# Attention in pairs of heads: three-pass scores issued in turn on the two 64-row halves of TensorE, in a two-block transformer on one core

## The chip, the core and the metric

The kernel runs on one core of a Trainium2 chip (trn2), in one launch. The metric is the device time of one execution in microseconds; the profiler's trace of one execution gives every instruction of the five engines: TensorE (PE, with its weight loads as PEld), VectorE (DVE), ScalarE (ACT), GpSimd (POOL) and SyncE (SP), which issues the transfers.

## The reference

Two transformer blocks of two layers each, in float32, on one sequence of 512 tokens of width 1024. The first block mixes a pooled branch, a convolved branch and dilated attention, then attends to a memory of 256 rows, then runs a gated MLP. The second attends with 512 tokens and 256 context rows; its layer 0 has grouped attention (A) and differential attention (B), its layer 1 windowed attention with a sink (C) and neighbourhood attention with a bias (D). Cut to the attention, all heads being 64 wide:

```python
def block(bi):                                   # block 1: 4 heads per group, 3 groups share one softmax
    for g, (window, dil) in enumerate(DIL_CONFIGS):
        sc = einsum("bhqd,bhqkd->bhqk", qb[g], kk) * scale
        ...
    wts = softmax(stack(lses, axis=0), axis=0)
    return sum(wts * stack(outs, axis=0), axis=0)
def gqa_attend(q, k, v):                         # A: 8 query heads on 2 key heads
    p = softmax(einsum('bqkgd,bskd->bkgqs', q, k), axis=-1)
    return einsum('bkgqs,bskd->bqkgd', p, v)
def diff_attend(q, k, v, lam):                   # B: 4 heads, two score maps each
    p = softmax(einsum('bqhjd,bshjd->bhjqs', q, k), axis=-1)
    return einsum('bhqs,bshe->bqhe', p[:, :, 0] - lam * p[:, :, 1], v)
# C: keys of 3 neighbouring blocks of 128 and the context, with a sink; D: 8 rows by 16 columns, with a bias
```

## The kernel before

Tokens lie in four blocks of 128 (`NB`), the context in two. Nearly all large products are made in three passes (`mm3`, lines 228 to 232): each operand is split into a part h and a rest l of type float32r, and h·h, l·h and h·l are added up in PSUM. These products are L230, L231 and L232 in the trace.

An attention is a list of **units** of three steps each, which `pipe` (line 401) puts into the program: `s` (scores and softmax, which leaves p [128 queries, keys] in SBUF), `t` (`keys_T`, line 380: TensorE transposes p in tiles of 128 into a PSUM tile of four, ACT or DVE copies it to SBUF) and `v` (`pv`, line 394: value products of two heads, one on each half of the array's columns). Before the change a unit is **one head** of one block of 128 queries; `lag` and `order` say how many units later its `t` and `v` follow. `mix` (line 77) lays other products, the fill, between the units, in a proportion from CONFIG: the gates of the first branch in block 1 (`gate_pass`), the projections of B beside A (`proj_b`), those of D beside C (`proj_d`), and beside B and D the first half of the output product (`out_first`), a token block of 24 products as soon as its attention is done. Tile's scheduler then puts the instructions of each engine into their final order.

A PSUM tile for scores, `wide` ([128, 1024], two buffers), holds one head. The scores are made in three ways:

- Block 1 (`attend`, lines 682 and 684), B (`attend_b` by `scores`, lines 1392, 1393 and, for context queries, 1395), the context's A (`attend_actx`, line 1470) and D (`attend_d` by `scores`): plain float32 products with 64 rows of contraction. A float32 product stands in the trace as two instructions.
- A and C (`s2`, lines 1336 and 1337): h and l of q lie stacked over the 128 rows, and meet a copy of h of k on both halves; then h of q meets l of k on 64 rows.

B and D differ in their softmax. In D two DVE passes (lines 1615 and 1618) add bias and mask, write p to SBUF and give the maximum; ACT takes the exponentials from p (line 360), DVE divides (lines 366 and 367). In B DVE reads the scores for the maximum (line 1507), ACT reads them once more for the exponentials (line 1510), DVE makes p0/d0 - lam·p1/d1 (lines 1511 to 1516). In B a second list of units, four of the context's A and then eight of the context's B, is interleaved one by one with the sixteen units of the tokens (`run`, line 1815).

Of the kernel before, what the change touches and what calls it, by code (L numbers as in the profile page):

```python
# [19 lines left out]
P = 128  # L20
D = 1024
# [13 lines left out]
CONFIG = dict(wm0=5,wm1=0,wm2=2,wm3=0,wm4=0,s1=16,s2=1,mixo0=20,mixo1=25,so=2,st=2,sf=8,d_e1=60,d_e2=60,shp=0,d_hn=25,eva=0,evb=0,evc=0,o1=0,om=0,oa=2,oc=3,evd=1, own=4, fa=40, fc=10, w1=2, slack=8, sm=4, sr=1, d_sub=110, mix1=125, mixm=130, laga=3, lagc=3, lag1=2, lagm=1, mixa=100, mixc=130, sz0=[6, 4, 4, 4, 4], sz1=[6, 4, 4, 4, 4], tick=60, bg=1500, d_mem=180, d_wmo=130, d_wout=180, d_in=60, d_ffn=80, d_op=60, d_opc=80, d_mlp=130, d_mlpc=120, d_last=140, d_ctx=100, d_rope=40, d_head=110, d_mod=100, raw=4, w=4, t4=6, a4=18, mm=4, wide=2)  # L35
# [23 lines left out]
class Act(list):  # L59
    """k-tiles (h, l) of an operand; ready(b) emits what token block b still waits for"""  # L60
# [16 lines left out]
def mix(main, fills, ahead=0.0):  # L77
    """runs main to its end; of each (gen, ratio) in turn about ratio microseconds for each of main's, after ahead of them"""
    fills = list(fills)
    b = 0.0  # L80
    while b < ahead:
        b += next(fills[0][0], ahead)
    a = b = 0.0
    for c in main:
        a += c
        while fills and b < fills[0][1] * a:
            d = next(fills[0][0], None)
            if d is None:
                fills.pop(0)
                a = b = 0.0  # L90
                break
            b += d


class Core:
    def __init__(self, nc, tc, es, I):
# [17 lines left out]
        self.spare, self.lent = [], {}  # L114
# [5 lines left out]
    def pe(self, us):  # L120
        """us of PE work were emitted; work that was put off until now follows"""
# [21 lines left out]
    def act(self, hl):  # L143
        """the k-tiles of a (h, l) pair of tiles whose blocks arrive under one key"""
# [14 lines left out]
    def t4(self, n=1024, dt=F32):  # L159
        if self.spare and n <= 768 and dt == F32:  # L160
            base = self.spare.pop(0)
            t = self.ap.tile([P, n], dt, tag="t4", name="t4", bufs=CONFIG["t4"]) if base is None else base[:, :n]
            self.lent[id(t)] = t, base
            return t
# [14 lines left out]
    def lend(self, tags=("hTh", "hTl")):  # L179
        """the memory of other tags as further t4 tiles; free() after their last use"""  # L180
        for tag in tags:
            t = self.ap.tile([P, 5, 768], F32, tag=tag, name=tag, bufs=1)
            self.spare += [t[:, i] for i in range(5)]
        self.spare += [None] * CONFIG["own"]

    def free(self, t):
        if id(t) in self.lent:
            self.spare.append(self.lent.pop(id(t))[1])

# [7 lines left out]
    def sm(self, n=1):  # L197
        return self.sp.tile([P, n], F32, tag=f"sm{n}", name=f"sm{n}", bufs=24 if n == 1 else 6)
# [15 lines left out]
    def w(self, src, k0, nk, c0, ncol):  # L214
        nc = self.nc
        raw = self.wp.tile([P, nk, ncol], F32, tag="wraw", name="wraw", bufs=CONFIG["raw"])
        nc.sync.dma_start(
            out=raw, in_=src[k0 * P:(k0 + nk) * P, c0:c0 + ncol].rearrange("(k p) n -> p k n", p=P)
        )
# [61 lines left out]
    def gained(self, y, g, out, eng=None):  # L281
        """(y * g, sum of squares of y over D) of one half"""
# [4 lines left out]
    def postnorm(self, x, parts):  # L287
        """x += rms(y) * g, the halves of y as gained() left them"""
# [10 lines left out]
    def fm(self, src, col, act, n=T):  # L299
        """feature-major product of one block of 128 columns: psum [128, n]"""  # L300
# [13 lines left out]
    def fm_halves(self, src, cols, act):  # L314
        """the same for several blocks of columns, the first half of the tokens before the second"""
# [12 lines left out]
    def tm_into(self, ps, ws, act, b):  # L328
        """token-major product of token block b: act[k] (h, l) [128, tokens], ws pieces of kpp k-tiles"""
# [9 lines left out]
    def tm_w(self, src, nk, c0, n):  # L339
        z = 2 if n > 256 else 4  # L340
        return [self.w(src, k, z, c0, n) for k in range(0, nk, z)]

    def tm(self, src, c0, n, acts, evac, between=None, ws=None):
        """acts: [(act, blocks, base)], in order"""
# [12 lines left out]
    def exp_norm(self, p, src, nmx, extra=None):  # L357
        nc = self.nc
        den = self.sm()
        nc.scalar.activation(p, src, AF.Exp, bias=nmx, scale=1.0, accum_out=den)  # L360
        if extra is not None:
            es = self.sm()
            nc.scalar.activation(es, extra, AF.Exp, bias=nmx, scale=1.0)
            nc.vector.tensor_add(den, den, es)
        rd = self.sm()
        nc.vector.reciprocal(rd, den)
        nc.vector.tensor_scalar(p, p, rd, None, op0=ALU.mult)

    def softmax2(self, p, S, nmx, den, n):
        """two rows of n keys side by side"""  # L370
# [9 lines left out]
    def keys_T(self, p, n):  # L380
        nc = self.nc
        pT = self.t4(n * P)
        for a in range(0, n, 4):
            b = min(a + 4, n)
            pt = self.ps1((b - a) * P)
            for m in range(a, b):
                nc.tensor.transpose(pt[:, blk(m - a)], p[:, blk(m)], self.ident)
            if a == 0 or self.evac:
                nc.scalar.copy(pT[:, a * P:b * P], pt)
            else:  # L390
                nc.vector.tensor_copy(pT[:, a * P:b * P], pt)
        return pT
# [1611 lines left out]
```

## Time and profile before

| | |
|---|---|
| time, median of 3 runs (lowest to highest) | 3663.67 us (3659.64 to 3666.01) |
| profiled execution, first to last instruction | 3659.7 us |
| what lies around that span in the median | 4.0 us |
| granted TensorE clock, mean | 0.989 of full |
| TensorE busy | 3557.6 us, 97% |
| VectorE, ScalarE, GpSimd busy | 2070.1, 1524.2, 490.7 us (57%, 42%, 13%) |
| transfers | 362.11 MB, 99 GB/s |

The page gives no separate time for the profiled execution; its span stands beside the median of the other runs. Matmuls are pipelined: one that is listed with 0.39 us may be followed by the next after 0.23 us, so what a matmul costs is read from the start of one to the start of the next. The attentions are five stretches of the span: block 1 at 152 us and 1113 us (two layers), A from 2019 us, B from 2164 us, C from 2983 us, D from 3136 us.

### The profile page before, as it was taken

How to read it: one execution, taken by the hardware profiler on the slowest of the kernel's cores; microseconds unless marked ns; L12 is line 12 of the kernel's file. 1: busy time of each engine (PE TensorE's matmuls, PEld its weight loads, DVE VectorE, ACT ScalarE, POOL GpSimd, SP SyncE). 2: the span in 40 equal slices, each digit the busy share in tenths (PEclk: the TensorE clock that was granted, in tenths of full speed). 3: DMA queues.
4: the chain of work that ended last, by engine and by line, in shares of the span. 5: the costliest groups of instructions: out<-in, count | busy, mean ns of one | idle time of the engine just before them, and what ended most of it. 6: DMA issues, size and time to landing. Idle time of an engine off the chain costs nothing. (4 is left out here: it accounts for less than half of the span.)

```text
span 3659.7 us, 47457 instructions
## 1 busy us (share of the span) xinstructions
PE 3557.6 (97%) x18504; PEld 2921.8 (80%) x18504; DVE 2070.1 (57%) x3329; ACT 1524.2 (42%) x2728; POOL 490.7 (13%) x463
## 2 busy tenths in 40 slices
PE   8999989999999999999999999999999999999999
PEld 7878878888797888888877776798888777668887
DVE  6655687576655436545676466644343664654445
ACT  4543455444544324443434454432222354554222
POOL 1222141123321011000023000200000110110000
PEclk9999999999999999999999999999999999999999
DMA  5434553444452234333441000322121320113332
GB/s 166 146 98 127 176 167 96 123 151 154 147 162 77 83 97 163 101 94 109 123 138 53 29 24 1 98 87 64 58 70 58 127 64 24 64 64 98 98 98 81
DMA packets 382096, 362.11 MB, mean 99 GB/s; under 512 B 20488, under 2 KB 297480, under 8 KB 381872
## 3 DMA queue, kind: packets, MB, share of 16 engines
q1 hardware_dynamic: 381872, 359.08, 31.2%
q8 instruction: 145, 2.38, 0.3%
q14 instruction: 79, 0.65, 0.1%
HBM read 347.34 MB, written 11.70 MB: 98 GB/s over the span
## 5 line engine op out<-in xcount | busy, mean ns | idle before, releaser
L225 DVE TENSOR_TENSOR wl<-wraw,wh 128x1024 fp32r<-128x1024 f32 (+2 forms) x499 | 612.0, 1231 | 616.4 <-ACT wh L221 613.4
L221 ACT CAST wh<-wraw 128x1024 fp32r<-128x1024 f32 (+2 forms) x504 | 510.2, 1016 | 789.1 <-PE mm L231 402.9
L230 PE MATMUL mm<-hTh,wh 128*128 128x512 f32 (+1 forms) x2112 | 785.7, 372 | 6.5 <-ACT hTh L237 4.4
L231 PE MATMUL mm<-hTl,wh 128*128 128x512 f32 (+1 forms) x2112 | 782.9, 371 | 2.0 <-DVE hTl L238 2.0
L232 PE MATMUL mm<-hTh,wl 128*128 128x512 f32 (+1 forms) x2112 | 782.7, 371 | 0.0
L230 PE MATMUL mm<-wh,a 128*128 128x512 f32 x1312 | 517.5, 395 | 3.0 <-DVE acc L1780 1.7
L231 PE MATMUL mm<-wl,a 128*128 128x512 f32 x1312 | 512.6, 391 | 1.1 <-DVE wl L225 1.1
L232 PE MATMUL mm<-wh,a 128*128 128x512 f32 x1312 | 511.7, 391 | 1.1 <-DVE a L238 1.1
L230 PEld LDWEIGHTS mm<-hTh,wh 128*128 128x128 f32 x2112 | 399.2, 189 | 76.6 <-ACT hTh L237 4.8
L232 PEld LDWEIGHTS mm<-hTh,wl 128*128 128x128 f32 x2112 | 399.7, 189 | 68.0
L231 PEld LDWEIGHTS mm<-hTl,wh 128*128 128x128 f32 x2112 | 399.8, 189 | 67.7 <-DVE hTl L238 2.4
L230 PEld LDWEIGHTS mm<-wh,a 128*128 128x128 f32 x1312 | 247.3, 189 | 62.4 <-issue 5.8
L232 PEld LDWEIGHTS mm<-wh,a 128*128 128x128 f32 x1312 | 246.9, 188 | 54.8 <-DVE a L238 2.9
L231 PEld LDWEIGHTS mm<-wl,a 128*128 128x128 f32 x1312 | 247.3, 188 | 51.6 <-DVE wl L225 2.2
L231 PE MATMUL mm<-wl,hTh 128*128 128x384 f32 (+2 forms) x640 | 226.5, 354 | 14.9 <-DVE wl L225 14.7
L230 PE MATMUL mm<-wh,hTh 128*128 128x384 f32 (+2 forms) x640 | 232.1, 363 | 4.0 <-ACT wh L221 2.5
L252 POOL TENSOR_TENSOR sm<-sm,mhalf 128x1 f32<-128x1 f32 (+3 forms) x112 | 83.6, 747 | 1097.5 <-DVE sm L248 783.3
L232 PE MATMUL mm<-wh,hTl 128*128 128x384 f32 (+2 forms) x640 | 226.0, 353 | 1.4 <-DVE hTl L238 1.4
L1096 ACT ACTIVATE t<-t,mod_s 128x512 f32<-128x512 f32 x168 | 119.7, 722 | 138.5 <-DVE macc L1092 69.3
L1097 POOL TENSOR_TENSOR t<-t,t 128x512 f32<-128x512 f32 x84 | 124.3, 1480 | 288.8 <-ACT t L1096 253.3
L1097 POOL TENSOR_TENSOR macc<-macc,t 128x512 f32<-128x512 f32 x84 | 120.9, 1440 | 311.8 <-ACT t L1096 257.8
L1780 DVE TENSOR_TENSOR acc<-acc,mm 128x512 f32<-128x512 f32 x112 | 76.8, 686 | 120.4 <-PE mm L232 120.2
(319 smaller groups left out, 5290.0 us busy)
## 6 DMA issues: line engine op xcount, KB each, us to landing
wraw<-in_w_in SPq DMA_DIRECT2D x108, 512.0 KB
t<-in_w_mod SPq DMA_DIRECT2D x96, 512.0 KB
wraw<-in_w_up SPq DMA_DIRECT2D x88, 512.0 KB
wraw<-in_w_mlp_in SPq DMA_DIRECT2D x64, 512.0 KB
wraw<-in_w_mlp_out SPq DMA_DIRECT2D x64, 512.0 KB
wraw<-in_w_down SPq DMA_DIRECT2D x44, 512.0 KB
a<-dr SPq DMA_DIRECT2D x38, 512.0 KB
wraw<-in_w_in SPq DMA_DIRECT2D x48, 384.0 KB
```

The source lines that it names most:

```text
L221: nc.scalar.copy(h, raw)
L225: eng.tensor_sub(l, raw, as32(h))
L230: mm(out, L[0], R[0], start=first, stop=False)
L231: mm(out, L[0], R[1], start=False, stop=False)
L232: mm(out, L[1], R[0], start=False, stop=last)
L252: nc.gpsimd.tensor_tensor(r, v, self.mhalf.to_broadcast([P, n]) if n > 1 else self.mhalf, op=ALU.pow)
L1096: nc.scalar.activation(w[:, kk], w[:, kk], AF.Copy, scale=sc)
L1097: nc.gpsimd.tensor_add(acc, acc, w[:, kk])
L1780: nc.vector.tensor_add(y, y, ps)
```

## The change

Heads are taken in pairs everywhere. A unit is now **two heads** (in B: the two score maps of one head), which lie on rows 0 to 63 and 64 to 127 of the array. Their scores are made in three float32r passes, for both in turn (`pair_scores`, the products at line 365 of the changed kernel), into both `wide` tiles. Both softmaxes, all their transposes (line 395; copies at lines 398, DVE, and 400, ACT) and their value products (line 409) belong to the one unit.

```diff
+    def pair_scores(self, S, segs):
+        for c0, n, q, k in segs:
+            for i, j in ((0, 0), (0, 1), (1, 0)):
+                for e in range(2):
+                    z = slice(64 * e, 64 * e + 64)
+                    self.nc.tensor.matmul(S[e][:, c0:c0 + n], q[i][z], k[j][z], start=i == 0 and j == 0, stop=i == 1)
+    def exp2(self, p, src, nmx, extra=None):
+        den = self.sm(2)
+        for e in range(2):
+            nc.scalar.activation(p[e], src[e], AF.Exp, bias=nmx[:, e:e + 1], scale=1.0, accum_out=den[:, e:e + 1])
...
+        nc.vector.reciprocal(den, den)
+        for e in range(2):
+            nc.vector.tensor_scalar(p[e], p[e], den[:, e:e + 1], None, op0=ALU.mult)
...
     def attend(self):
...
-                        S = c.ps2()
-                        nc.tensor.matmul(S[:, 0:512], qT[0][q0, hp, blk(r)], kT[0][q0, hp], start=True, stop=True)
-                        for g in (1, 2):
-                            nc.tensor.matmul(S[:, 384 + 128 * g:512 + 128 * g], qT[g][q0, hp, blk(r)], kT[g][q0, hp, blk(r)],
-                                             start=True, stop=True)
+                S = [c.ps2(), c.ps2()]
+                segs = []
+                for g in range(3):
+                    k = kT[hp][g] if g == 0 else tuple(z[:, blk(r)] for z in kT[hp][g])
+                    segs.append(((0, 512, 640)[g], (512, 128, 128)[g], (t[:, 0, g], t[:, 1, g]), k))
+                c.pair_scores(S, segs)
...
     def attend_b(self, outs, blocks, key, done=None):
...
+                    for j in range(2):
+                        nc.vector.tensor_reduce(nmx[:, j:j + 1], S[j][:, :n], axis=AX, op=ALU.max, negate=True)
+                    for j in range(2):
+                        nc.scalar.activation(p[j], S[j][:, :n], AF.Exp, bias=nmx[:, j:j + 1], scale=1.0, accum_out=den[:, j:j + 1])
+                    nc.vector.reciprocal(den, den)
+                    nc.vector.tensor_mul(den[:, 1:2], den[:, 1:2], self.nlam)
+                    nc.scalar.activation(p[1], p[1], AF.Copy, scale=den[:, 1:2])
+                    nc.vector.scalar_tensor_tensor(p[0], p[0], den[:, 0:1], p[1], op0=ALU.mult, op1=ALU.add)
...
     def attend_d(self, outs, done):
...
+                    for e in range(2):
+                        nc.vector.tensor_tensor_reduce(out=p[e][:, :512], in0=S[e][:, :512],
...
+                        nc.vector.tensor_tensor_reduce(out=p[e][:, 512:], in0=S[e][:, 512:768], in1=self.band[:, 3 * P:5 * P],
...
+                    nc.vector.tensor_scalar(mx, mx, -1.0, None, op0=ALU.mult)
+                    c.exp2(p, p, mx)
...
     def w(self, src, k0, nk, c0, ncol, pairs=False):
+        if pairs and k0 < 4:
+            for e in range(2):
+                r0 = 256 * e + 64 * k0
+                nc.sync.dma_start(out=raw[64 * e:64 * e + 64],
+                                  in_=src[r0:r0 + 64 * nk, c0:c0 + ncol].rearrange("(k p) n -> p k n", p=64))
```

With it go: keys kept as h and l (block 1 splits them in `qkv`, B after its projections into the memory of hTh and hTl, D in `proj_d`); queries split shortly before use (`split_t4`, one split for several units); no stacked copies for A and C; rows of w_out reordered by half tiles (eight more transfers in all); in block 1 `pool_mix` ahead of the last projections. In CONFIG each lag is 1 instead of 1 to 3 units, the order of the steps is v, t, s, `t4` has 10 buffers instead of 6 and borrows none from hTh and hTl, and bits say which copy of transposed tiles DVE makes (in block 1, A, C and D the second of each unit, in B none). The number of TensorE instructions in the program goes from 17,234 to 17,874, of DVE's from 3,331 to 3,204, of ACT's from 2,318 to 2,309; POOL's 468 are the same.

The order on TensorE in block 1, layer 0, before; `wide` numbers are heads, `t4` are p tiles:

```order
L682 MATMUL wide_1701<-a4_164,a4_161 128x512
L684 MATMUL wide_1701<-a4_165,a4_162 128x128
L684 MATMUL wide_1701<-a4_166,a4_163 128x128
L387 MATMUL mm_1716<-ident_72,t4_1614 128x128 x4
L387 MATMUL mm_1722<-ident_72,t4_1614 128x128 x2
L682 MATMUL wide_1726<-a4_164,a4_161 128x512
L684 MATMUL wide_1726<-a4_165,a4_162 128x128
L684 MATMUL wide_1726<-a4_166,a4_163 128x128
L399 MATMUL mm_1740<-t4_1638,a4_167 64x128
L399 MATMUL mm_1740<-t4_1715,a4_167 64x128
```

and in the changed kernel, where equal rows are merged:

```order
L395 MATMUL mm<-ident,t_1702 128x128 x6
L395 MATMUL mm<-ident,t_1703 128x128 x6
L365 MATMUL wide<-a_709,t_1714 128x512 x6
L365 MATMUL wide<-a_710,t_1714 128x128 x6
L365 MATMUL wide<-a_711,t_1714 128x128 x6
```

The three products of one head are now eighteen of two heads in turn, and both heads' transposes stand together.

The order on DVE in D, before (ISA rows with a `t4` are the passes of lines 1615 and 1618):

```order
L366 RECIPROCAL sm1_26012<-sm1_26010 128x1
L1615 ISA t4_26061,sm1_26062<-wide_26058,hTl_25628 128x512
L1615 ISA sm1_26062 128x1
L367 TENSOR_SCALAR t4_26003<-t4_26003,sm1_26012 128x768
L1618 ISA t4_26061,sm1_26063<-wide_26058,phase2_14507,sm1_26062 128x256
```

and in the changed kernel (lines 1599 and 1602 are these passes, 380 divides, 398 copies transposed tiles):

```order
L1602 ISA t4_25986,sm2_25988<-wide_25972,phase2_14643,sm2_25987 128x256
L1602 ISA sm2_25988 128x1
L1605 TENSOR_SCALAR sm2_25988<-sm2_25988 128x2
L378 RECIPROCAL sm2_25994<-sm2_25994 128x2
L380 TENSOR_SCALAR t4_25985<-t4_25985,sm2_25994 128x768
L380 TENSOR_SCALAR t4_25986<-t4_25986,sm2_25994 128x768
L398 COPY t4_26012<-mm_26019 128x512
L1599 ISA t4_26046,sm2_26048<-wide_26032,hTh_25742 128x512
```

Before, the next head's first pass (26061) stood ahead of the division of this one (26003); now the next pair's passes (26046) stand behind this pair's division and behind the copy of its transposed tiles.

The order on TensorE in B of the changed kernel, where units of the tokens (768 keys) and of the context's queries (256 keys) alternate; line 1515 holds the value products:

```order
L365 MATMUL wide_18504<-hTh_17689,t4_18429 128x256
L365 MATMUL wide_18504<-hTl_17690,t4_18429 128x256
...
L395 MATMUL mm_18494<-ident_72,t4_18480 128x128 x4
L395 MATMUL mm_18500<-ident_72,t4_18480 128x128 x2
L1515 MATMUL mm_18452<-a4_17093,t4_18493 128x128 x2
...
L365 MATMUL wide_18541<-hTh_17689,t4_18145 128x512
L365 MATMUL wide_18542<-hTh_17689,t4_18145 128x512
...
L1515 MATMUL mm_18490<-a4_17095,t4_18536 128x128 x2
L365 MATMUL wide_18585<-hTh_17689,t4_18429 128x256
...
L395 MATMUL mm_18575<-ident_72,t4_18557 128x128 x4
```

Between the scores of a tokens' unit (18541, 18542) and its transposes (t4_18557) stand two value products and the six scores of a context's unit; before, heads of two units and fill stood there.

## Rows read from the trace of the kernel before

**Rows 1.** Page, part 1: busy us (share), instructions of TensorE; loads overlap.
```profile
PE 3557.6 (97%) x18504; PEld 2921.8 (80%) x18504; DVE 2070.1 (57%) x3329; ACT 1524.2 (42%) x2728; POOL 490.7 (13%) x463
```

**Rows 2.** Windows: us, busy (x) of PE, PEld, DVE, ACT, POOL; clock; DMA share; GB/s.
```profile
152.00:270.00 118.00, 117.07 (x688) 88.89 (x686) 72.03 (x137) 58.45 (x96) 23.57 (x18) 1.00 0.33 100
...
2019.00:2163.00 144.00, 144.00 (x904) 107.35 (x904) 77.18 (x142) 66.48 (x125) 5.29 (x3) 1.00 0.09 30
2163.00:2318.00 155.00, 149.43 (x797) 99.78 (x793) 108.11 (x235) 77.22 (x201) 5.03 (x5) 0.96 0.09 29
...
2983.00:3132.00 149.00, 147.17 (x883) 112.53 (x882) 70.61 (x217) 67.13 (x160) 9.23 (x5) 1.00 0.15 50
3132.00:3265.00 133.00, 129.63 (x850) 85.71 (x849) 75.84 (x243) 72.38 (x159) 11.20 (x7) 0.97 0.11 39
```

**Rows 3.** Timeline, TensorE, one head of block 1: start, us, line, form, count.
```profile
152.44 1.12 PE L682 MATMUL wide<-a,a 64*128 64x512 f32 x2
153.41 0.60 PE L684 MATMUL wide<-a,a 64*128 64x128 f32 x4
153.94 0.50 PE L230 MATMUL mm<-hTh,wh 128*128 128x512 f32 x1
```

**Rows 4.** Timeline, TensorE, block 1, where two heads meet.
```profile
162.61 0.27 PE L684 MATMUL wide<-a,a 64*128 64x128 f32 x1
162.62 0.69 PE L682 MATMUL wide<-a,a 64*128 64x512 f32 x1
162.72 0.49 PE L684 MATMUL wide<-a,a 64*128 64x128 f32 x3
```

**Rows 5.** Timeline, TensorE, first and last of 19 dense products.
```profile
154.75 0.39 PE L230 MATMUL mm<-hTh,wh 128*128 128x512 f32 x1
...
158.84 0.39 PE L230 MATMUL mm<-hTh,wh 128*128 128x512 f32 x1
```

**Rows 6.** Timeline, TensorE, one head of attention C, 640 keys.
```profile
3000.59 0.42 PE L1336 MATMUL wide<-a,a 128*128 128x384 f32 x1
...
3001.31 0.38 PE L1336 MATMUL wide<-a,a 128*128 128x256 f32 x1
3001.62 0.38 PE L1337 MATMUL wide<-a,a 64*128 64x256 f32 x1
3001.94 0.66 PE L387 MATMUL mm<-ident,t 128*128 128x128 f32 x4
```

**Rows 7.** Timeline, TensorE, block 1: value products, transposes, next product.
```profile
176.21 1.53 PE L399 MATMUL mm<-t,a 128*64 128x128 f32 x24
177.68 0.88 PE L387 MATMUL mm<-ident,t 128*128 128x128 f32 x6
178.31 0.48 PE L230 MATMUL mm<-hTh,wh 128*128 128x512 f32 x1
```

**Rows 8.** Timeline, attention D, softmax of a head on DVE and ACT.
```profile
3190.31 0.67 DVE L1615 CUSTOM_DVE_ANT_0 t<-wide,hTl 128x512 f32<-128x512 f32 x1
...
3190.90 0.62 DVE L367 TENSOR_SCALAR t<-t,sm 128x768 f32<-128x768 f32 x1
3191.43 0.48 DVE L1618 CUSTOM_DVE_ANT_0 t<-wide,phase,sm 128x256 f32<-128x256 f32 x1
...
3192.14 0.94 ACT L360 ACTIVATE t<-t,sm 128x768 f32<-128x768 f32 x1 [1.95 <-DVE sm L1620]
```

**Rows 9.** Timeline, attention B, all engines; brackets: idle before, releaser.
```profile
2208.16 0.96 DVE L1507 TENSOR_REDUCE sm<-wide 128x1 f32<-128x768 f32 x1
...
2209.15 0.90 ACT L1510 ACTIVATE hTl<-wide,sm 128x768 f32<-128x768 f32 x1 [1.45 <-DVE sm L1507]
...
2210.19 1.95 PE L1392 MATMUL wide<-a,a 64*128 64x512 f32 x2 [1.64 <-ACT hTl L1510]
...
2211.81 1.00 DVE L1516 SCALAR_TENSOR_TENSOR hTh<-hTh,sm,hTl 128x768 f32<-128x768 f32 x1
...
2213.41 0.63 PE L231 MATMUL mm<-wl,a 128*128 128x512 f32 x1
```

More of the change, by code (lines that the diff above doesn't have):

```diff
@@ new lines, in keys_T @@
+    def keys_T(self, ps, n):
+        nc = self.nc
+        todo = [p[:, blk(m)] for p in ps for m in range(n)]
+        out, held = [], []
+        for a in range(0, len(todo), 8):
+            part = todo[a:a + 8]
+            pT = self.t4(len(part) * P)
+            held.append(pT)
+            for b in range(0, len(part), 4):
+                z = part[b:b + 4]
+                pt = self.ps1(len(z) * P)
+                for i, t in enumerate(z):
+                    nc.tensor.transpose(pt[:, blk(i)], t, self.ident)
+                o = pT[:, b * P:(b + len(z)) * P]
+                if (self.evac >> ((a + b) // 4)) & 1:
+                    nc.vector.tensor_copy(o, pt)
+                else:
+                    nc.scalar.copy(o, pt)
+            out += [pT[:, blk(i)] for i in range(len(part))]
+        return [out[i * n:(i + 1) * n] for i in range(len(ps))], held
@@ L923, in run @@
             drain(self.pool(l, act))
+            for _ in range(2 * NB):
+                next(qkv)
+            drain(self.pool_mix(l))
             drain(qkv)
-            drain(self.pool_mix(l))
             acc = c.acc([KD, T])
@@ L1398, in ktiles, with gqa_units, prep, s @@
     def ktiles(self, b):
         return list(range(NB + NCB)) if b < NB else list(range(NB, NB + NCB))
-    def pair_units(self, blocks, score, vs, out, cost):
+    def gqa_units(self, outs, cost, soft, vrange):
         c = self.c
+        Q, k, va = self.A
+        c.need(("A",))
+        units, qs = [], {}
+        def prep(kt):
+            if kt < 4:
+                qs[kt] = c.split_t4([Q[0][kt // 2][:, kt % 2]], T)
+        for kt in range(4):
+            po = {}
+            for b in range(NB):
+                st = {}
+                def s(kt=kt, b=b, st=st):
+                    if kt == 0 and b == 0:
+                        prep(0)
+                    st["p"] = soft(kt, b, [c.ps2(), c.ps2()], [z[:, blk(b)] for z in qs[kt]], k)
+                    if b == 1:
+                        prep(kt + 1)
+                def t(st=st):
+                    p, n = st["p"]
+                    st["pT"], st["t"] = c.keys_T(p, n)
+                def v(kt=kt, b=b, po=po, st=st):
+                    if b == 0:
+                        po["t"] = c.ps1()
+                    c.pv(po["t"][:, blk(b)], st["pT"], [[va[:, m, HALF[e]] for m in vrange(b)] for e in range(2)])
+                    if b == NB - 1:
+                        f = outs(kt)
+                        c.split(f[0], f[1], po["t"])
+                units.append((cost, s, t, v))
+        return units
@@ L1491, in attend_b, with prep @@
         c, nc = self.c, self.c.nc
-        qb, kb, vb = self.B
-        c.need(("B",))
-        units = []
+        qb, K, vb = self.B
+        units, qs = [], {}
+        def prep(b):
+            if b in blocks:
+                src = [z[:, :, blk(b)] for z in qb[0]] if b < NB else [qb[1][:, :, blk(b - NB)]]
+                qs[b] = [z.rearrange("p (h t) -> p h t", h=4) for z in c.split_t4(src, 4 * P)]
         for b in blocks:
             po = {}
+            x0, n = (0, KEYS) if b < NB else (T, CTX)
@@ new lines, in t, with v @@
+                def t(n=n // P, st=st):
+                    (st["aT"],), _ = c.keys_T([st["p"]], n)
+                def v(b=b, h=h, st=st, po=po):
+                    if h == 0:
+                        po["t"] = c.ps1()
+                    ks = self.ktiles(b)
+                    for i, m in enumerate(ks):
+                        nc.tensor.matmul(po["t"][:, blk(h)], st["aT"][i], vb[m // 2][:, m % 2, blk(h)],
+                                         start=i == 0, stop=i == len(ks) - 1)
+                    if h == 3:
+                        self.subnorm(po["t"], b - blocks[0], outs, key)
+                        if done is not None:
+                            done.append(b)
@@ L1539, in attend_b @@
+                units.append((3.1 if b < NB else 1.1, s, t, v))
         return units
@@ L1651, in attend_d @@
+                units.append((4.0, s, t, v))
         return units
```

510 lines of the change are left out of this document (190 added, 320 removed).

## Prediction

> **What bounds the kernel now.** First the page's busy shares: TensorE is busy 97% of the span, every other engine under 60% [rows 1]. Then the windows of the attentions: there too TensorE is nearly full (117.1 of 118 us in block 1, 144 of 144 in A, 147.2 of 149 in C, 129.6 of 133 in D); only in B do others come near, with DVE at 108.1 of 155 and the clock at 0.96 [rows 2]. Whatever leaves TensorE there shortens the program, until a chain of DVE and ACT that TensorE now covers comes to light. So I price the products first and then look, attention by attention, at what else lies between one unit and the next. About 0.2% (7 us) is the least that a measurement of this kernel can tell from no change.
>
> **What a pair of heads costs TensorE now.** One head of block 1 takes from 152.44 to 153.94, 1.50 us for 768 keys [rows 3]: 3.0 us a pair, and the same in B and D, whose heads have as many keys and are float32 products too. One head of C with 640 keys takes from 3000.59 to 3001.94 [rows 6]: 2.7 us a pair; with the other half of C's blocks (512 keys, 0.31 us for each of four products) 2.6 on average, and in A with 768 some 2.9.
>
> **What it will cost.** Eighteen dense products follow each other in 158.84 - 154.75 = 4.09 us, 0.227 us per 512 columns and pass [rows 5]. If the two halves of the array run side by side, a pair of 768 keys costs 3 x 1.5 x 0.227 = 1.02 us; if they run one after the other, 2.04. Rows 4 show which: the last products of a head on one half start at 162.61, 162.72 and on, while the other head's first starts on the other half at 162.62 and isn't held up [rows 4]. I take them as side by side. Products of 256 columns on 128 and on 64 rows in turn take 0.31 us where 0.227/2 = 0.11 would do [rows 6], so a change of array shape costs up to 0.2; the changed kernel pays it about once per unit, not at each product. I take 1.2 us a pair (bounds 1.02 and 2.04 + 0.4 = 2.45), in C with 576 keys on average 1.0. The saving on TensorE is then 16 x 1.8 = 29 us in block 1 (eight pairs in each of two layers), 16 x 1.7 = 27 in A, 16 x 1.6 = 26 in C, 29 in B and 29 in D, and some 10 for the context's twelve units: 150 us, which would be 4%.
>
> The Trainium skill ("TensorE: Matmul & The Clock Gate", Measured speedup vs the span model) has four row tiles gain a factor of 3.07, not 4. Held against a pair this would make 1.02 into 1.33 us and take some 13 us from the savings of block 1, A and C; rows 4 show no such loss for two halves, and I stay with them.
>
> **How much of it stays.** Transposes and value products are as many as before: six transposes take 178.31 - 177.68 = 0.63 us, the value products of a pair 1.47 [rows 7], together 1.26 + 1.47 a pair, so a unit without fill holds about 4 us of TensorE. What must fit beside it is its softmax.
>
> *Block 1.* Each unit has one gate of fill, 33 products of 0.227 = 7.5 us, between its scores and its transposes. Two DVE passes, two exponentials and a division, about 5.5 us by the lengths in [rows 8], are covered. Small products of 128 columns may be held by their weight loads (four lie in 0.53 us in [rows 3]), so I book 25 of the 29.
>
> *A.* In the new order ten units have 24 products (5.45 us) of fill, six have none. In these the next scores wait until ACT has read both `wide` tiles, and the unit takes some 6 us instead of 4: 27 - 12 = 15.
>
> *C.* All but two units have 24 products; 26 - 3 = 23.
>
> *D.* Here the fill is thin: 67 products among sixteen units, 74 before. The order on DVE decides. Before, a head's first pass stood ahead of the division of the head before it, so DVE worked while ACT did. Now DVE goes through a whole pair: four passes (0.59 from start to start for 512 columns, about 0.40 for 256: 2.0 us), 0.23 to the first exponential, then it waits for two exponentials (0.94 and a read of the sum, together 1.04 each: 2.1), the reciprocal 0.1, two divisions 0.62 + 0.53, then for the transposes of the second head's first tiles (about 0.5) and its copy (about 0.67, as a pass of 512 columns), and only then come the next pair's passes [rows 8]. The sum is 6.7 us, more than TensorE's 5 with its fill. Sixteen of these (107), 8 us for the ends and some 6 of neighbouring work that the window of D holds make 121 against its 133 [rows 2]: 12 less, of which 7 fill products left for later give back 1.6. I book 10 of the 29.
>
> *B.* Both `wide` tiles belong to one pair, and the shown order puts little between a unit's scores and its transposes. Per tokens' unit: two maxima 0.95 + 0.9, the second exponential 1.04 (its maximum read at 2209.15, TensorE released at 2210.19), 0.3 for the small ones, the scaled copy on ACT about 0.8 (no row has it; the exponential, 0.90, is nearest; 0.6 to 0.94 are its bounds), the last DVE operation 1.00 [rows 9]: 5.1 us from scores to transposes. Then 0.65 of transposes, 0.6 of copy, 0.7 of value products and 1.7 for the next scores with what stands among them: 9.1 us a turn with a context's B unit, eight turns. With a unit of the context's A, whose two maxima and four exponentials must be read before the next tokens' scores, I count 12.5, four turns; the last four units about 6.2. With 12 us for ends and the norm of each block, and 5 of neighbouring work, this is 50 + 73 + 25 + 12 + 5 = 165, where the window of B has 155 [rows 2]. 24 fill products less among them (48, not 72) cost 5.4 later. So B gives nothing, and costs some 15. That is the working in which I trust least: 0 to 45.
>
> *The rest.* Eight more transfers of half the size: SP's queue is far ahead of TensorE in B and D (DMA share 0.09 and 0.11 in [rows 2]), no cost. More splits of keys on ACT and DVE in the projections: DVE is 53% busy where TensorE is full [rows 2], no cost; if that cover were gone, each would cost about 0.6 us.
>
> The sum: -25 - 15 - 23 - 10 + 15 = -58. From the profiled span of 3659.7 us this gives 3601.7, and with the 4.0 us by which the median lies above that span **3606 us**.
>
> **Rivals.** *All waits are covered* (0.13): DVE and ACT work ahead of what I read, and all of the products' 150 us stay, 3664 - 150 = 3514. For it: both have room over the whole span [rows 1]. Against: in D and B the chain goes through single buffers and a fixed order. *The halves don't run side by side in float32r* (0.10): rows 4 show it for float32 products, which move columns half as fast. Then a pair costs 1.0 more: 16 each in block 1 and A, 12 in C, and about 15 in B and D, 59 in all, and the time is 3666, no change. *Slower, by the clock* (0.17): after an idle stretch of 1.64 us in B the trace has products of 512 columns at 0.63 us instead of 0.39, and the window's clock at 0.96 instead of 1.00 [rows 2, 9]: the lower level, 1.2 GHz. In D TensorE would be busy 5 of 6.7 us, in B 4 of 9. At the lower level D's 5 us become 10, and its sixteen units 160 us instead of 107, which makes +43 of the -10; in B some 3.3 us of each turn's chain double, 54 in all on top of the 15. With -25 - 15 - 23 the sum is +49, 3713. It decides once B and D run more than half their time at that level; at half of it the change is worth nothing (3660). Against it: dilated work fills the gaps, and the clock came back within B before.
>
> **The numbers.** The forecast itself gets 0.60, with 3606 and, from B's 0 to 45, D's -29 to +5 and 10 us in the others, 3570 to 3650 of its own. Range 3550 to 3670: it leaves out most of the full gain and of the slow case. Faster: 0.60 x 0.95 + 0.13 and 0.04 from the milder ends of the other two, 0.74; same 0.10, mostly the second rival; slower 0.16.
>
> **What would show it.** In the profile after: first and second half's products of 512 columns starting within 0.02 us of each other, a block-1 pair in 1.2 to 1.5 us; D's units 6.7 us apart with DVE idle for ACT between the passes and the reciprocal; B's turns near 9 us with TensorE idle before its transposes, and B no shorter than 150 us. A pair at 2.4 us would say that the halves take turns; B or D at TensorE's own 4 to 5 us a unit that I counted waits that the order hides; a clock under 0.8 in either that the slow rival is right.

## The result and the profile after

| | before | changed |
|---|---|---|
| time, median (lowest to highest) | 3664.62 us (3659.64 to 3666.01), 4 runs | 3700.28 us (3696.58 to 3705.47), 4 runs |
| ratio to before, 95% interval | | 1.010 (1.0085 to 1.0114) |
| span of the profiled execution | 3659.7 us | 3697.9 us |
| granted TensorE clock, mean | 0.989 | 0.970 |

The change makes the kernel about 1% slower, where 3606 us was forecast. The page of the changed kernel, part 1 and the row of the clock in part 2:

```profile
PE 3506.6 (95%) x18888; PEld 2942.8 (80%) x18888; DVE 2076.9 (56%) x3202; ACT 1536.9 (42%) x2719; POOL 491.7 (13%) x463
...
PEclk9999989999999999999999977899999999899999
```

Beside [rows 1] TensorE is busy 51 us less, and still the span is 38.2 us longer: the savings are there, and waits have taken more. The clock falls to 0.7 to 0.8 in four slices past the middle, three of them together (B) and one later (D).

Both kernels issue the same 14,160 dense three-pass products in the same order, so the two spans can be cut at the same products. Cut so, the stretches are block 1's projections and attention in layers 0 and 1, A while it has fill, A's end with B, C, and D. Windows of the kernel before (columns as in [rows 2]):

```profile
107.40:284.00 176.60, 175.67 (x997) 140.35 (x996) 111.71 (x209) 88.50 (x151) 36.44 (x27) 1.00 0.39 120
1067.80:1258.10 190.30, 190.09 (x1057) 153.19 (x1056) 95.53 (x197) 81.37 (x139) 18.05 (x16) 1.00 0.33 97
2018.70:2136.50 117.80, 117.80 (x698) 88.67 (x697) 57.03 (x106) 51.06 (x97) 5.29 (x3) 1.00 0.06 19
2136.50:2327.70 191.20, 185.63 (x1045) 126.75 (x1044) 130.64 (x277) 95.23 (x238) 11.52 (x10) 0.96 0.11 37
2989.10:3124.50 135.40, 135.40 (x817) 104.13 (x816) 62.50 (x202) 60.12 (x140) 1.73 (x1) 1.00 0.14 47
3124.50:3268.40 143.90, 140.53 (x915) 94.30 (x914) 83.30 (x254) 77.72 (x167) 19.21 (x11) 0.98 0.13 46
```

and of the changed kernel:

```profile
106.90:275.70 168.80, 165.78 (x1044) 138.26 (x1043) 118.36 (x203) 90.47 (x155) 37.71 (x28) 0.99 0.40 126
1063.50:1245.80 182.30, 178.84 (x1105) 149.94 (x1105) 101.25 (x194) 86.58 (x148) 19.51 (x17) 1.00 0.34 101
2004.20:2115.60 111.40, 108.72 (x786) 87.63 (x785) 60.91 (x93) 57.56 (x107) 5.28 (x3) 1.00 0.07 20
2115.60:2370.10 254.50, 194.07 (x1118) 151.17 (x1117) 121.18 (x241) 121.89 (x293) 12.21 (x10) 0.79 0.09 27
3031.80:3154.80 123.00, 119.92 (x876) 98.40 (x875) 66.55 (x166) 56.72 (x137) 0.93 (x1) 0.99 0.15 48
3154.80:3308.00 153.20, 123.41 (x978) 97.52 (x977) 95.15 (x242) 70.11 (x136) 20.84 (x11) 0.91 0.14 46
```

The first column after the window is its length. Block 1 gains 7.8 + 8.0, A 6.4, C 12.4; D loses 9.3, and A's end with B loses 63.3 at a clock of 0.79. What lies outside these stretches adds up to next to nothing: 38.2 + 15.8 + 6.4 + 12.4 - 9.3 - 63.3 = 0.2. Block 1's gain is uncertain: in the traces of the experiments in which block 1 is the same, its two stretches gain 9 to 14 us together.

**The halves do run side by side.** TensorE's timeline of a block-1 pair (start, us, line, form, count; the first row is a narrow window on the start of the second):

```profile
203.10 0.50 PE L365 MATMUL wide<-a,t 64*128 64x512 f32 x2
...
203.10 1.58 PE L365 MATMUL wide<-a,t 64*128 64x512 f32 x18
...
204.62 0.50 PE L220 MATMUL mm<-hTh,wh 128*128 128x512 f32 x1
```

Two products of 512 columns end 0.50 us after the first began, as long as one alone. The pair takes 204.62 - 203.10 = 1.52 us, where two heads of [rows 3] take 3.0.

**What B waits for.** Waits of TensorE in B (the waiting line, what it waited for, us in all, times, longest):

```profile
PE mm L395 <- DVE t L1502: 31.5, 13, 4.7
PE wide L365 <- ACT t L1498: 12.3, 12, 2.2
```

One turn there, a tokens' unit and a context's B unit, with all engines (brackets: idle before, releaser):

```profile
2247.46 1.02 DVE L1502 SCALAR_TENSOR_TENSOR t<-t,sm,t 128x768 f32<-128x768 f32 x1
2248.53 1.12 PE L395 MATMUL mm<-ident,t 128*128 128x128 f32 x4 [1.98 <-DVE t L1502]
2249.68 0.59 ACT L400 COPY t<-mm 128x512 f32<-128x512 f32 x1 [2.26 <-PE mm L395]
2250.17 0.48 ACT L1498 ACTIVATE t<-wide,sm 128x256 f32<-128x256 f32 x1
...
2250.81 2.77 PE L1515 MATMUL mm<-a,t 128*128 128x128 f32 x12
...
2253.50 0.79 PE L365 MATMUL wide<-hTh,t 64*128 64x512 f32 x2
...
2256.10 1.82 DVE L1496 TENSOR_REDUCE sm<-wide 128x1 f32<-128x768 f32 x2 [2.59 <-PE wide L365]
```

Read downwards, it is one chain: last DVE operation, transposes, their copy, value products, and only then (2253.50) the next tokens' scores, with DVE idle for 2.59 us until they are there. From one last DVE operation to the next, tokens' units are 17.0 us apart with a context's A unit (2151.90 to 2219.84, four turns), 13.9 with a context's B unit (to 2330.64, eight turns) and 6.1 alone (to 2348.88, three turns). In these last turns the scheduler has put the next scores ahead of the transposes:

```profile
2336.36 0.77 PE L365 MATMUL wide<-hTh,t 64*128 64x512 f32 x2
...
2338.03 0.88 PE L395 MATMUL mm<-ident,t 128*128 128x128 f32 x6
```

**What D waits for.** The waits in D, and a turn:

```profile
PE mm L395 <- DVE t L380: 26.7, 15, 3.0
```

```profile
3204.70 1.32 PE L365 MATMUL wide<-a,t 64*128 64x512 f32 x12
3204.82 0.94 ACT L372 ACTIVATE t<-t,sm 128x768 f32<-128x768 f32 x1 [1.46 <-DVE sm L1605]
...
3206.80 0.17 DVE L378 RECIPROCAL sm<-sm 128x2 f32<-128x2 f32 x1 [2.02 <-ACT t L372]
3207.00 1.15 DVE L380 TENSOR_SCALAR t<-t,sm 128x768 f32<-128x768 f32 x2
3207.77 1.50 PE L395 MATMUL mm<-ident,t 128*128 128x128 f32 x12 [1.75 <-DVE t L380]
...
3208.87 0.69 DVE L398 COPY t<-mm 128x512 f32<-128x512 f32 x1 [0.72 <-PE mm L395]
...
3209.48 0.68 DVE L1599 CUSTOM_DVE_ANT_0 t<-wide,hTh 128x512 f32<-128x512 f32 x1
...
3212.60 0.93 ACT L372 ACTIVATE t<-t,sm 128x768 f32<-128x768 f32 x1 [0.83 <-DVE sm L1605]
```

DVE idles 2.02 us for the exponentials and 0.72 for the transposes. The next pair's scores (3204.70) are made long before its first pass (3209.48); ahead of that pass stand, on DVE, this pair's division and the copy of its transposed tiles. This turn takes 7.78 us; the sixteen units are 7.0 to 8.2 us apart.

### The profile page after: what moved, and what is told of

Its sections match the earlier page's. It is cut to its first block, busy times and chain, and to the rows that moved or that the text cites. A ratio compares the mean times of both kernels' runs of the same rounds, so it can differ in the third digit from the quotient of the medians.

```text
span 3697.9 us, 47989 instructions
## 1 busy us (share of the span) xinstructions
PE 3506.6 (95%) x18888; PEld 2942.8 (80%) x18888; DVE 2076.9 (56%) x3202; ACT 1536.9 (42%) x2719; POOL 491.7 (13%) x463
## 5 line engine op out<-in xcount | busy, mean ns | idle before, releaser
L220 PE MATMUL mm<-wh,a 128*128 128x512 f32 x1280 | 503.2, 393 | 3.4 <-DVE acc L1753 2.0
L221 PE MATMUL mm<-wl,a 128*128 128x512 f32 x1280 | 499.6, 391 | 1.4 <-DVE wl L215 1.4
L222 PE MATMUL mm<-wh,a 128*128 128x512 f32 x1280 | 498.5, 391 | 1.0 <-DVE a L228 1.0
L220 PEld LDWEIGHTS mm<-wh,a 128*128 128x128 f32 x1280 | 240.9, 188 | 57.9 <-ACT a L227 3.2
L222 PEld LDWEIGHTS mm<-wh,a 128*128 128x128 f32 x1280 | 240.6, 188 | 52.8 <-DVE a L228 2.8
L395 PE MATMUL mm<-ident,t 128*128 128x128 f32 x928 | 142.4, 300 | 73.5 <-DVE t L1502 36.5
L395 PEld LDWEIGHTS mm<-ident,t 128*128 128x128 f32 x928 | 112.1, 152 | 100.4 <-issue 62.7
L400 ACT COPY t<-mm 128x512 f32<-128x512 f32 (+1 forms) x185 | 100.4, 551 | 171.0 <-PE mm L395 170.3
```

The source lines that it names most:

```text
L220: mm(out, L[0], R[0], start=first, stop=False)
L221: mm(out, L[0], R[1], start=False, stop=False)
L222: mm(out, L[1], R[0], start=False, stop=last)
L395: nc.tensor.transpose(pt[:, blk(i)], t, self.ident)
L400: nc.scalar.copy(o, pt)
```

## The experiments

Two theories stood after this reading. **Order** (theory 1 in the expectations): with the steps v, t, s at a lag of one unit, little stands between a unit's scores and its transposes where there is no fill, so its softmax stands bare on the path. **Clock** (theory 2): TensorE drops to 1.2 GHz in the gaps, and its doubled work is the loss. Each run is compared with 3700 us; runs without an interval are single executions.

### b_order: B in the order s, v, t

```diff
+        self.order = None
         for u in chain(units, [None] * (lag + 1)):
+            order = order if self.order is None else self.order
...
             c.evac = CONFIG["evb"]
+            c.order = 0
```

> Only the order of the steps in B changes: scores of a unit, then value products, then the transposes of the unit before (s, v, t); until now v, t, s. Theory 1 (order: one unit's softmax stands bare on the path, because its transposes and their copies on ACT come ahead of the next unit's exponentials): the turns of 13 us with a context's B unit fall to about 9, the first four from 17 to about 13; 8 x 4.4 + 4 x 4 = 51, so 3650 us (3640 to 3670), and TensorE's clock in B rises from 0.76 to above 0.9. Theory 2 (clock: TensorE drops to 1.2 GHz in gaps, and its doubled work is what B loses): gaps stay where a pair holds both score tiles, 3690 to 3705. Rival 3 (both score tiles taken by one pair: the next scores wait for the exponentials whatever the order): at most 12 us, the wait of the scores for ACT, are not won and the transposes' wait moves to the scores: 3685 to 3700.

Measured: 3636.0 us, 64 less. The window of A's end and B, and the wait of the transposes:

```profile
2114.00:2308.50 194.50, 170.12 (x1118) 133.16 (x1117) 119.12 (x241) 119.37 (x293) 11.57 (x10) 0.93 0.11 36
```

```profile
PE mm L395 <- DVE t L1504: 1.0, 1, 1.0
```

The same instructions take 194.5 us instead of 254.5, the clock comes back to 0.93, and the wait of the transposes for the last DVE operation goes from 36.5 us (31.5 in B, 5.0 at its first unit) to 1.0. The theory of the order holds. It does not yet say how much of the 60 us was the clock.

### b_copy: B's copies of transposed tiles on DVE

One entry of CONFIG:

```diff
-evb=0
+evb=3
```

> Only the engine of the copies of transposed tiles in B changes, ACT to DVE. Theory 1 (order): the context unit's exponentials no longer stand behind a copy on ACT that waits for the tokens' transposes (2.3 us of ACT's wait per turn), but its last DVE operation now stands behind that copy on DVE: 1 to 2 us of the turns of 13 us, 8 to 16 in all, 3685 to 3692. Theory 2 (clock): nothing on TensorE changes, 3700 within 5.

Measured: 3705.5 us, nothing won; the small gain that the theory of the order expected did not come. Timeline of a turn:

```profile
2256.47 0.46 ACT L1498 ACTIVATE t<-wide,sm 128x256 f32<-128x256 f32 x1
...
2257.67 1.11 PE L395 MATMUL mm<-ident,t 128*128 128x128 f32 x4 [1.98 <-DVE t L1502]
...
2262.75 0.79 PE L365 MATMUL wide<-hTh,t 64*128 64x512 f32 x1
```

The context's exponentials now start 1.2 us ahead of the tokens' transposes, and the next tokens' scores come no sooner: they stand behind transposes and value products in TensorE's own queue. It is that queue's order that matters, not ACT's.

### b_dummy10, b_dummy20, b_dummy30: the clock held by products that nobody reads

```diff
+                    if n == KEYS:
+                        d = c.ps1()
+                        for i in range(10):
+                            nc.tensor.matmul(d, q[0], K[0][:, h, :T], start=True, stop=True)
```

(20 and 30 in the other two.)

> Ten products of 512 columns that nobody reads (2.3 us at the higher clock) are added after the scores of each tokens' unit in B, into a PSUM tile of their own; all else as in the changed kernel. They fill about the mean wait of the transposes for the last DVE operation (31.5 us in 13 waits, 2.4 each). Theory 2 (clock): the granted clock in B rises from 0.76 to above 0.9, the doubled work of TensorE falls away, and B gets 25 to 45 us shorter: 3655 to 3675. Theory 1 (order): the clock may rise, but the chain of DVE and ACT sets the turn: 3690 to 3715.

> The same with twenty products (4.5 us at the higher clock, about the longest of these waits), so that TensorE has hardly a gap left before the transposes. Theory 2 (clock): the clock in B above 0.95; what it gives back (25 to 45 us) is met by 16 x 2.1 = 34 us by which the products are longer than the mean wait: 3690 to 3710. Theory 1 (order): the 34 us are added to 3700 with little back: 3720 to 3740.

> Thirty products nobody reads after each tokens' scores in B, order v, t, s as in the changed kernel. With twenty the transposes started 0.06 to 0.4 us behind the last DVE operation in most turns, so twenty about fill the bare chain at the higher clock. Theory 1 with that reading: ten more add 16 x 2.3 = 36 us less some 3, 3712 to 3718. If the twenty still hid in a longer gap (the clock the larger part of the loss): 3682 to 3700.

Measured: 3695.9, 3682.5 and 3716.2 us. With ten, A's end and B take 246.3 us at a clock of 0.89. The window with twenty, and one of its turns:

```profile
2116.50:2357.90 241.40, 225.20 (x1437) 178.84 (x1436) 121.98 (x241) 123.10 (x293) 11.56 (x10) 0.99 0.09 29
```

```profile
2227.14 1.02 DVE L1506 SCALAR_TENSOR_TENSOR t<-t,sm,t 128x768 f32<-128x768 f32 x1 [1.07 <-ACT t L1505]
...
2230.25 1.50 PE L1519 MATMUL mm<-a,t 128*128 128x128 f32 x12
...
2231.68 0.51 PE L365 MATMUL wide<-hTh,t 64*128 64x512 f32 x2
...
2234.07 4.83 PE L1496 MATMUL mm<-hTh,t 128*128 128x512 f32 x20
...
2238.41 1.02 DVE L1506 SCALAR_TENSOR_TENSOR t<-t,sm,t 128x768 f32<-128x768 f32 x1 [0.39 <-ACT t L1505]
...
2239.72 0.66 PE L395 MATMUL mm<-ident,t 128*128 128x128 f32 x4
```

With twenty the clock is 0.99, and the stretch still takes 241.4 us: 13 less than 254.5. The added products cost some of that. In the sixteen tokens' units the transposes started 9.5 us in all behind the end of the last DVE operation, against 3.1 in the changed kernel (each less 0.1 for the signal). And the last three turns, without a context's unit, take 24.5 us instead of 18.2, since the scheduler put the next scores behind the transposes there (2321.43 and 2322.23); under 2 us of these 6 are in the starts just counted. So with the clock held and nothing added the stretch would take, by estimate, some 230 to 241 us. Of the 63 us lost, **13 to 24 are the clock's and 39 to 50 the chain's**. With thirty the stretch takes 32 us more than with twenty, nearly the 36 us of 160 further products: twenty had just filled the bare chain. Each theory was right in a part. Ten and thirty came where the theory of the order put them. Twenty came out under both ranges, nearer to that of the clock: the clock gave back more than the theory of the order granted, and the added products cost less than either had booked.

### b_lag2: another unit in between, the order kept

One entry of CONFIG, which holds for A and B:

```diff
-laga=1
+laga=2
```

> The steps stay in the order v, t, s, but in A and B the lag is 2 units instead of 1: another unit's scores stand between a unit's scores and its transposes. Theory 1 (what is lost in B is that nothing stands between them): nearly what the order s, v, t gave there, 3640 (3632 to 3655). Rival (it is the place of the scores ahead of the transposes in the queues, not the distance): under 20 us won, 3680 to 3700.

Measured: 3634.6 us, as with the other order. A, A's end and B take 303.3 us together, 305.9 in b_order, 365.9 in the changed kernel, 309.0 before. So what was missing in B is any work between scores and transposes; by which edit it gets there is the same. The lag is part of the change: in the kernel before, transposes in A to D followed three units, of one head each, behind their scores; in the changed kernel they follow one pair behind.

### b_late and order_dummy: what is left in B

In b_late, B in the order s, v, t, the reciprocal, the scaled copy and the last DVE operation are put off too, into a function `div` that the transposes call (its definition is left out here):

```diff
                 def t(n=n // P, st=st):
+                    st["div"]()
                     (st["aT"],), _ = c.keys_T([st["p"]], n)
```

> B in the order s, v, t, and the reciprocal, the scaled copy on ACT and the last DVE operation put off to the transposes, so that on ACT the next unit's exponentials come ahead of this unit's scaled copy. The run with the order alone gave 3636 us and left 24 us of TensorE's waits in A's end and B, 8.4 of them for copies on ACT. Theory 1: what is left is now the units' own work; the exponentials come earlier and the score tiles come free earlier, but the transposes come later: 3625 to 3640. Rival: the chain from the exponentials to the transposes stands bare again because it now starts a step later: 3645 to 3665.

In order_dummy six products that nobody reads follow each tokens' scores, in that order:

> B in the order s, v, t, with six products nobody reads (1.4 us) after each tokens' scores. Theory 1 (order; the clock is a consequence): the 27 us at 1.2 GHz left in A's end and B shrink to under 10, which gives back at most 10; the 16 x 1.4 = 22 us of the products are added where TensorE is now nearly full: 3640 to 3655, slower than 3636. Theory 2 (the clock is what is left to win): 3625 to 3635.

Measured: 3641.5 and 3647.2 us, 5.5 and 11 more than b_order. The late division fell between its two expectations: nothing won. With six products the stretch takes 200.1 us at a clock of 0.95, 5.6 more than 194.5: once the order is mended, the clock that is left is not worth buying with such products.

### d_order, d_late: D

The first puts `c.order = 0` at D as b_order does at B, the second puts off the division as well.

> Only the order of the steps in D changes, from v, t, s to s, v, t. Theory 1 (a pair's softmax stands bare between its scores and its transposes): in D the turns are 7.0 to 8.2 us, the chain of DVE (four passes, wait for two exponentials, two divisions, a copy that waits for the transposes) with 26.7 us of waits of the transposes. With the next scores ahead of the transposes the passes no longer wait for transposes and scores; DVE's own passes, the wait for the exponentials and the divisions, 5.6 us with the copy at most 6.3, remain: 16 x 1 to 2, so 3670 to 3685. Rival 3 (DVE's order alone counts: the passes stand behind the division anyway): 3695 to 3702, no change.

> As the run before, and the division of a pair is put off to its transposes, so that on DVE the next pair's passes come ahead of it, as in the kernel before. Theory 1: DVE now works while ACT takes the exponentials; a turn needs some 4.3 us of DVE and 4.0 of ACT beside 4.5 to 5 of TensorE: from 7.5 to about 5 us, 16 x 2.5 = 40, 3660 (3650 to 3672), and the clock in D rises from 0.91 to 0.97 or more. Rival 3 (order of the steps is enough): the same as the run before within 5 us.

Measured: 3668.1 and 3671.3 us; the 32 us of d_order are a little more than theory 1 had. The window of D in d_order, and one turn:

```profile
3152.40:3276.40 124.00, 111.33 (x978) 88.81 (x977) 93.15 (x242) 68.63 (x136) 21.35 (x11) 0.96 0.18 56
```

```profile
3203.80 0.94 ACT L372 ACTIVATE t<-t,sm 128x768 f32<-128x768 f32 x1
...
3204.72 1.31 PE L365 MATMUL wide<-a,t 64*128 64x512 f32 x12
...
3207.04 0.68 DVE L1601 CUSTOM_DVE_ANT_0 t<-wide,hTl 128x512 f32<-128x512 f32 x1
...
3207.43 1.09 PE L395 MATMUL mm<-ident,t 128*128 128x128 f32 x8
...
3209.61 0.94 ACT L372 ACTIVATE t<-t,sm 128x768 f32<-128x768 f32 x1 [0.90 <-DVE sm L1607]
3209.81 0.69 DVE L398 COPY t<-mm 128x512 f32<-128x512 f32 x1
```

D takes 124.0 us instead of 153.2, and this turn 5.8. The cause is not B's. On TensorE the next pair's scores stood ahead of the transposes in the changed kernel too (3204.70 and 3207.77), as they do here (3204.72 and 3207.43). What differs is DVE's order: the passes (3207.04) now come right behind the division, and the copy of the transposed tiles, which waits for TensorE, behind them (3209.81). The waits of the transposes for the division fall from 26.7 to 7.7 us. No run moves that copy alone in the order v, t, s, so this reading rests on the rows.

My further step in d_late, the passes ahead of the division, wins nothing: 3671.3 us lies at the end of theory 1's range, but the turns of 5 us that it promised did not come, and D takes 124.5 us, as in d_order. At 5.8 us DVE, 93 of 124 us busy, and TensorE, 111 of 124, leave little to win.

### one_head: three passes of one half, then of the other

```diff
-            for i, j in ((0, 0), (0, 1), (1, 0)):
-                for e in range(2):
+            for e in range(2):
+                for i, j in ((0, 0), (0, 1), (1, 0)):
```

> In the scores the loop over the two heads goes outside the loop over the three passes: all three passes of one half, then of the other, no longer in turn. Theory A (the halves run side by side only when products for them alternate in the queue): a pair of block 1 costs 3 x 0.33 or so more, 16 x 1.0 in block 1, 16 in A, 12 in C, with B and D partly hidden behind their chains: 3740 to 3760. Theory B (TensorE overlaps them whatever the order, by some depth of its queue): 3700 within 6.

Measured: 3699.4 us, no change. The program has them in threes,

```order
L365 MATMUL wide_1682<-a4_709,t4_1601 128x512 x3
L365 MATMUL wide_1683<-a4_709,t4_1601 128x512 x3
```

and the timeline of a pair in block 1 shows

```profile
205.39 0.50 PE L365 MATMUL wide<-a,t 64*128 64x512 f32 x2
...
206.91 0.51 PE L220 MATMUL mm<-hTh,wh 128*128 128x512 f32 x1
```

Products still start in twos (the trace does not name the half), and the pair still takes 206.91 - 205.39 = 1.52 us. "Issued in turn" is no condition for running side by side, at least with three in a row.

### bd_order, all_order, all_order_1, all_order_act and best: the order everywhere

bd_order has both edits; all_order sets `oa=0, oc=0`, so A and C too; all_order_1 also `o1=0`, block 1; all_order_act is all_order with `evd=0`, D's copies on ACT. best is all_order_1 again, timed.

> The order s, v, t in both B and D, the rest as in the changed kernel. Theory 1 (order): the two gains are in different stretches and add up: 3700 - 64 - 32 = 3604 (3597 to 3611), 1.6% faster than the kernel before. Theory 2 (a time given to one stretch is taken back by the clock in the next): less than the sum, 3615 to 3640.

> The order s, v, t in all four attentions of the second block, A and C too. Theory 1 (order): where fill lies between scores and transposes nothing is won, but A's last six units and C's last two have none, and TensorE waits there some 7 and 3 us in the run with B's order alone: 3604 - 5 to 10, so 3595 to 3600. Rival: A and C with fill lose, since a unit's fill now stands behind its transposes' partner and not before them: 3604 to 3615.

> As the run before, and block 1 in that order too. All of block 1's units have 7.5 us of fill between scores and transposes: no change of more than 3 us either way by either theory, except that the first pair's transposes come one step later: 0 to 3 us.

> As the run with A to D in the order s, v, t, and D's copies of transposed tiles all on ACT instead of one in three on DVE. Theory 1 says of D that DVE's order decides: the copy, which waits for the transposes, stands ahead of the next pair's passes; without it DVE's turn loses 0.7 us and its wait for the transposes: up to 16 x 1 us less than that run. Rival: ACT, with 2.1 us of exponentials and then three copies of 0.6, becomes the one that is late: the same or up to 10 us more.

> The order s, v, t in all five attentions again, timed in rounds, to tell whether the one look of 3594.5 holds. Theory 1: block 1's order gives 3 us or less, 3600 within 4. If that look was right, the transposes in block 1 waited for something that the trace of the changed kernel shows only as the first pair's late start: 3593 to 3597.

| kernel | time | ratio to before (95%) |
|---|---|---|
| bd_order | 3609.4 us (3608.3 to 3611.1) | 0.9851 (0.9834 to 0.9867) |
| all_order | 3603.0 us (3601.5 to 3604.2) | 0.9834 (0.9820 to 0.9849) |
| all_order_1 | 3594.5 us, one execution | |
| all_order_act | 3604.1 us, one execution | |
| best | 3600.7 us (3595.7 to 3607.1) | 0.9828 (0.9815 to 0.9842) |

The two gains add up. A and C in that order give some 6 us more, between the two expectations of all_order; in the two profiled executions C is 3.6 us shorter, A with its end and B only 0.6, and the rest lies where both programs are the same. Block 1's single execution of 3594.5 did not hold: its order is worth nothing that these runs tell. D's copy on ACT changes nothing, where theory 1 had up to 16 us: the passes stand ahead of that copy in the order s, v, t already. In best, A's end with B takes 188.1 us and D 126.0, against 191.2 and 143.9 in the kernel before.

So the change is worth 1.7%, 63 us, in the order s, v, t; in the order with which it came it costs 1%. What the pairs alone are worth is not shown: lag, copies and buffers changed with them.

## Why the prediction was wrong

**Sign and size.** 3606 us was forecast and 3700 measured, above the range. By the terms of the sum (A's -15 held its last six units too, which are measured with B):

| term | booked | measured |
|---|---|---|
| block 1, both layers | -25 | -15.8 |
| A (with fill) | -15 | -6.4 |
| C | -23 | -12.4 |
| D | -10 | +9.3 |
| B (with A's end) | +15 | +63.3 |

**The failed step is B's turn**: "9.1 us a turn with a context's B unit, eight turns", and 12.5 with a context's A unit. Measured are 13.9 and 17.0. (The terms shown for the 9.1 add up to 8.75; the difference is small beside the miss.) From the last DVE operation to the end of the next scores I had booked 0.65 + 0.6 + 0.7 + 1.7 = 3.65 us; in the turn shown it is 2248.48 to 2256.0, 7.5, with 6.6 of them at 1.2 GHz, and 5.9 in b_dummy20 at the higher level (2228.16 to 2234.07). Even there each term is longer: transposes and copy 2.1 us instead of 1.25, value products 1.4 instead of 0.7, the next scores with the context's transposes among them 2.4 instead of 1.7. I had put one chain into a turn, and the context's unit beside it; on TensorE part of that unit stands in the chain. The clock makes it worse, but with the clock held (b_dummy20) the tokens' last DVE operations are still 12.3 us apart in those eight turns (2214.6 to 2312.7, their ends). The softmax itself was counted nearly rightly, 5.1 us from scores to transposes: in b_dummy20 it is 2234.07 to 2239.43, 5.4. That the last units came as forecast, 6.2 and 6.1 us, is in part luck, since the scheduler put their scores ahead of the transposes. I had called this the working I trusted least, and still bounded it at 45 us.

**D**: the mechanism came as forecast, four passes, a wait for two exponentials, two divisions, a copy that waits for the transposes, with DVE idle at just these places. The period was sized 6.7 us; it is 7.0 to 8.2, 7.5 on average, in a stretch whose clock is 0.91. Over the fifteen distances that is 12 of the 19 us between -10 and +9.3; the others lie at the ends of the stretch, and I did not trace them.

**Block 1, A and C**: a pair costs 1.52 us, not 1.2. The 512-column products take the 0.23 us each that I used, but the first product costs 0.33 until the next starts, and the twelve of 128 columns take 0.11 a pair of halves, as long as whole 128-row ones. Sixteen times 0.3 is 5 of block 1's 9 us; the rest is, in the main, a wait of 1.8 us per layer of the first scores for their split queries, which I had not booked. In C the scores themselves fell from 36.8 to 18.5 us in the stretch (sums from start to start); 6 of these 18 us came back, 3.6 of them in the transposes, which waited 3.0 us for divisions. The Trainium skill ("TensorE: Matmul & The Clock Gate", Measured speedup vs the span model) has its factor of 3.07 for four row tiles; held against a pair, it gives an estimate of 1.33 us. The measured 1.52 lies beyond that, though the 512-column products of the two halves overlap fully, with starts 0.003 us apart.

**The rivals.** That the halves take turns is excluded. The slow rival had the right sign and place, and its +69 for B is close to +63. Its mechanism is the smaller part: 13 to 24 us of B are the clock's. The test that I had given for it, a clock under 0.8 in B or D, is met in B (0.79) and still misleads, since a bare chain lowers the clock as well (b_order adds no product and has 0.93); in D, with 0.91, it isn't met. What I had not set up as a rival is the one that decided: in B the order of the steps on TensorE leaves a pair's softmax bare. D's chain on DVE I had priced, somewhat short.

**Left open**: why in the changed kernel 4.7 us are lost between 489 and 620 us of the span, around the attention to the memory in block 1's layer 0, in a stretch with 20 us at 1.2 GHz against 10 before; the other runs show 0.2 to 4.3 there with the same instructions.

## What to carry to other kernels

Merging two units into one doubles the softmax that lies between a unit's first products and its dependent ones. Where there is no fill, issue the next unit's first products ahead of the dependent ones, or raise the lag by a unit, before judging such a change: here the same work takes 3700 or 3601 us. Look at every engine's order when you do: what was gained in D was gained on DVE. Where a stretch shows a low clock, hold it with products that nobody reads and see what remains, before blaming it.

## What the runs showed of the hardware

- Products on the two 64-row halves ran side by side in float32r, also where three of one half were issued ahead of three of the other (starts 0.01 us apart in one_head; 1.52 us a pair either way).
- A 128-column product on 64 rows takes 0.11 us from start to start beside its twin on the other half, as a 128-row one does (204.08 to 204.19 and 202.79 to 202.90 in the changed kernel).
- Twenty added products per unit made the program faster by 18 us (3682.5, one execution, against 3700): 13 of them lie in A's end with B, where the clock rose from 0.79 to 0.99.
